# The state-space coefficient moves from B's factors to the powers: one group of transposes, and another order of tables and first products

## The chip, the cores and the metric

The kernel runs on one core of one Trainium2 chip. A core has five engines that run side by side and wait for each other by semaphores: TensorE (PE, matrix products), VectorE (DVE), ScalarE (ACT), GpSimd (POOL) and SyncE (SP, which here only issues DMAs). The metric is the device time of the program in microseconds (us); smaller is better. The three runs of the kernel before took 1129.54, 1130.26 and 1454.06 us; their median is 1130.26 us.

## The reference

A trunk of two layers works on 1024 frames of width 1024. Layer 0 has two branches, a diagonal complex state-space layer (S5) with a GLU, and a retention with eight heads; layer 1 is a convolution module. Each layer is `x = x + mixer(rmsnorm(x))`, and a last RMSNorm follows. The change lies in the S5 part, which for 64 groups of 16 channels and 64 states computes

```
dt = exp(log_dt);  lb = exp((a_re + i a_im) * dt)          # one step of the state
coef = (lb - 1) / (a_re + i a_im)
bb = coef[..., None] * (b_re + i b_im)                     # (64 groups, 64 states, 16 channels)
s_t = lb * s_(t-1) + bb @ u_t                              # over all frames
y_t = Re(c @ s_t) + d * u_t
```

## The kernel before

**Layer 0's front.** `layer0_front` first brings in x, makes its scaled high and low parts (each product of layer 0 is three TensorE products of high and low parts, `mm3`), and computes blocks u0 to u7 of the input projection (`u_block`, 128 columns each, in two halves `mm_u<nb>_0` and `mm_u<nb>_1` of 24 products). Every block is scaled by DVE into a tile `ut` and written to memory as `u_d`. Then come the gate blocks g8 to g23 (`gate_block`, halves `mm_g<nb>_0` and `_1`), and between them the eight blocks B = 0 to 7 of the state-space layer, one for every two gate blocks.

**The state-space layer.** It works in groups of eight frames. `s5_params` makes, on DVE, the powers 0 to 8 of lb (`pr`, `pi`), the rotation factors for longer distances (`e1`, `e2`) and the coefficient (`cfr`, `cfi`); on POOL it makes bb (`s5_bbr`, `s5_bbi`) in six operations named s5bb and s_bb in the profile. `s5_turned` brings the powers and bb into another layout: ACT reorders bb into `hq`, PE transposes three groups of four 128x128 tiles (`turn0` for the powers, `turn1` and `turn2` for bb), ACT copies each group out of PSUM into a tile `turned`, and SP writes it to memory (`pt_d` for the powers, `bt_d` for bb). ACT also copies bb into `bd`, which the products kp read. For each block B, `s5_w2` loads four tiles from there, with rows repeated (PTr and PTi, BTr and BTi, 256 KB each), copies the powers to PSUM (`pw0`, `pw1`) and multiplies them complexly by bb with six DVE operations; the result W2 is what the products `v0`, `v1` of `s5_states` apply to the block's input U (loaded back from `u_d` by `s5_load`). `s5_tables` lets POOL make, in six operations each, W3 (powers times C, read by the products kp and y) and the rotation tables Tc and Ts (read by DVE behind v). `s5_states` issues v and kp and lets DVE add kp and d into Kg; `s5_scan` rotates v on DVE, scans it and rotates it back into S; `s5_out` issues the products y.

**What sets the order.** A scheduler places the instructions of each engine; where the order matters it is written out by hand, as pairs (late, early) of the n-th instruction that writes a named tile: the list `ORDER`, and the pairs that `s5_order` makes for DVE: in each block Kg, then the rotation of v (m0, m1) and the first six operations on v, then the gates and the next block's W2. On PE, `turn1` begins behind the last product of `mm_u6_0`, and v and kp of block 0 stand ahead of the seventh product of `mm_g8_0`. On an engine, and in SP's queue of DMAs, instructions run in order: one that waits holds up all behind it.

**Buffers.** Tiles live in pools that open and close. The pool `ev` (the early pool) holds x, temporaries, bb and the tiles `hq` and `turned`; it is closed after `s5_turned`, and the pool `s5w` of the state-space blocks (U, PT, BT, W2, W3, Tc, Ts and others) takes its place: a tile there waits for the last user of the tile that it lies over. `s5c` lives through the whole front, `mid` through front and retention.

Of the kernel before, what the change touches and what calls it, by code (L numbers as in the profile page):

```python
# [11 lines left out]
F32 = mybir.dt.float32  # L12
# [3 lines left out]
ALU = mybir.AluOpType  # L16
# [3 lines left out]
P = 128  # L20
# [20 lines left out]
ORDER = (  # L41
    ('PE', ('turn1', 0), ('mm_u6_0', 23)),
    ('DVE', ('W2r_0', 0), ('ut_7', 0)),
    ('DVE', ('kraw_3', 0), ('yn_2', 0)),
# [24 lines left out]
    ('PE', ('mm_g9_0', 0), ('kp_0', 7)),  # L69
    ('PE', ('mm_g8_0', 6), ('kp_0', 7)),  # L70
    ('Activation', ('wh_glu2', 0), ('rs_6_0', 0)),
# [13 lines left out]
def s5_order():  # L85

    seq = []
    for b in range(8):
        g, h = 8 + 2 * b, 9 + 2 * b
        turns = [(f"m0_{b}", 0), (f"m1_{b}", 0)]  # L90
        kern = [(f"Kg_{b}", 0), (f"Kg_{b}", 1)]
        z = [(f"v{c}_{b}", n) for n in range(4) for c in range(2)]
        back = [(f"d0_{b}", 0), (f"d1_{b}", 0), *z[6:], (f"S_{b}", 0), (f"S_{b}", 1)]
        w = [(f"{t}_{b + 1}", n) for t, n in (("W2r", 0), ("W2i", 0), ("pw0", 0), ("pw1", 0), ("W2r", 1), ("W2i", 1))]
        w = w if b < 7 else []
        seq += [*kern, *turns, *z[:6]]
        if b:
            seq += [*back, (f"gt_{g}", 0), (f"wl_g{h}", 0), *w[:3], (f"gt_{g}", 1), *w[3:]]
        else:
            seq += [(f"gt_{g}", 0), *w, *back, (f"gt_{g}", 1)]  # L100
        seq += [(f"gt_{h}", 0), *([(f"wl_g{g + 2}", 0)] if b < 7 else []), (f"gt_{h}", 1)]
    return [("PE", ("mm_g8_0", 6), ("v1_0", 7)),
            *(("Activation", (f"pw0_{b + 1}", 0), (f"gt_{8 + 2 * b}", 0)) for b in range(1, 7)),
            *(("DVE", late, early) for early, late in zip(seq, seq[1:]))]
# [33 lines left out]
class Trunk:  # L138
# [208 lines left out]
    def layer0_front(self, st):  # L347
# [144 lines left out]
        self.s5_tab, self.s5_back, self.s5_open, self.s5_last = {}, {}, {}, None  # L492
        for nb in range(3, 6):
            u_block(nb)
        self.s5_turned(ev)
        early.close()
        self.s5 = self.pool("s5w", 1, stack=st)
        self.s5_first = self.s5_load(0)
        for nb in range(6, 8):
            u_block(nb)  # L500
# [153 lines left out]
    def s5_params(self, sp, tp):  # L654
# [162 lines left out]
        with self.tc.issue_after(self.last_phase.ins):  # L817
# [20 lines left out]
            tt(cfi[:], a1[:], rden[:], ALU.mult)  # L838
        self.bb = [tp.tile([P, NP, 16], F32, name=f"s5_bb{c}") for c in "ri"]
        bc = lambda q: q[:].unsqueeze(2).broadcast_to([P, NP, 16])  # L840
# [26 lines left out]
    def s5_turned(self, pool):  # L867


        nc = self.nc  # L870
        self.pt_d = self.dram.tile([2, 2, P, P], F32, name="pt_d")
        self.bt_d = self.dram.tile([2, 4, P, P], F32, name="bt_d")
        fl = lambda t, a, n: t[:, a * n:(a + 1) * n, :].rearrange("p a b -> p (a b)")
        order = [pool.tile([P, 4, P], F32, name=f"hq{c}", tag="sq", bufs=2) for c in range(2)]
        for o, t in zip(order, self.bb):
            nc.scalar.copy(o[:].rearrange("p a (h q) -> p (a h) q", h=4), t[:].rearrange("p q h -> p h q"))
        for i, (dst, parts) in enumerate((
                (self.pt_d[:].rearrange("c a r n -> r (c a) n"), [fl(t, a, 4) for t in (self.pr, self.pi) for a in range(2)]),
                (self.bt_d[0].rearrange("a r n -> r a n"), [order[0][:, a, :] for a in range(4)]),
                (self.bt_d[1].rearrange("a r n -> r a n"), [order[1][:, a, :] for a in range(4)]))):  # L880
            ps = self.bank(f"turn{i}")
            for a, src in enumerate(parts):
                nc.tensor.transpose(ps[:, a * P:(a + 1) * P], src, self.ident[:])
            t = pool.tile([P, 4, P], F32, name=f"turned{i}", tag="xin", bufs=8)
            nc.scalar.copy(t[:].rearrange("p q n -> p (q n)"), ps[:])
            nc.sync.dma_start(dst, t[:])
        for q, t in zip(self.bd, self.bb):
            for g in range(2):
                r = slice(64 * g, 64 * g + 64)
                nc.scalar.copy(q[r, :, 16 * g:16 * g + 16], t[r])  # L890

    def s5_w2(self, B):

        nc, v = self.nc, self.nc.vector
        (ptr, pti), (btr, bti) = ([self.big(f"{n}{c}_{B}", f"{n}{c}", 1) for c in "ri"] for n in ("PT", "BT"))
        dp, db = self.pt_d, self.bt_d

# [22 lines left out]
    def s5_tables(self, B):  # L920
# [8 lines left out]
        pj = lambda t: t[:, :, qs].rearrange("p j q -> p q j").unsqueeze(3).broadcast_to([P, 4, 9, 16])  # L929
        W3 = w.tile([P, 2, 4, 9 * 16], F32, name=f"W3_{B}", tag="W3", bufs=2)  # L930
        made = [self.outer(B, W3[:, 0], W3[:, 1], pj(self.pr), pj(self.pi), bj(self.cr), bj(self.nci), vm,
                           ALU.add, ALU.subtract)]

        Tc, Ts = self.big(f"Tc_{B}", "Tc", 2), self.big(f"Ts_{B}", "Ts", 2)
        vt = lambda ap: ap.rearrange("p q (a b) -> p q a b", b=16)
        ea = lambda t: t[:, 0:8, qs].rearrange("p a q -> p q a").unsqueeze(3).broadcast_to([P, 4, 8, 16])
        eb = lambda t: t[:, 0:16, qs].rearrange("p b q -> p q b").unsqueeze(2).broadcast_to([P, 4, 8, 16])
        made.append(self.outer(B, Tc[:], Ts[:], ea(self.e2[0]), ea(self.e2[1]), eb(self.e1[0]), eb(self.e1[1]), vt))

        self.s5_last = self.chained(chain(*made), self.s5_last)  # L940
        R8 = self.big(f"R8_{B}", "R8", 1)
# [1049 lines left out]
def layout(inp):  # L1991
# [28 lines left out]
    A["s5_prm"] = np.stack([gn(inp["s5_a_re"][0]), gn(inp["s5_a_im"][0]), gn(ldt)], axis=1)  # L2020
    b = lambda a: a.reshape(32, 2, 64, 16).transpose(1, 2, 0, 3).reshape(P, 32, 16)
    c = lambda a: b(a.transpose(0, 2, 1))
    A["s5_br"], A["s5_bi"] = b(inp["s5_b_re"][0]), b(inp["s5_b_im"][0])
# [27 lines left out]
```

## Time and profile before

The profiled execution took 1130.23 us; its profile spans 1128.4 us of that.

| what | value |
|---|---|
| profiled execution, us | 1130.23 |
| its span, us | 1128.4 |
| median of the runs, us | 1130.26 |
| PE busy | 1113.1 us (99%) |
| PE weight load busy | 978.2 us (87%) |
| DVE busy | 816.0 us (72%) |
| ACT busy | 500.2 us (44%) |
| POOL busy | 593.1 us (53%) |
| mean rate of all DMAs | 233 GB/s |

Times in the profile are microseconds from the start of the span; "mean ns" is the duration of one instruction. Matmuls are pipelined, so the distance between two starts, not the duration shown, is what one costs. A row names the line of the kernel, the operation, the tile written and, behind the arrow, the tiles read; buffer and block numbers are left out, so `mm_u` stands for all u blocks. "idle before, releaser" is the time that the engine stood still just before the instruction, and the one that ended it. A DMA's row is its issue; when it has landed is seen from the instructions that waited for it.

### The profile page before, as it was taken

Reading aid. Unit: us, or ns where it says so; the run is one execution under the profiler, and the core shown is the slowest. Engines: PE = TensorE matmul, PEld = TensorE weight load, DVE = VectorE, ACT = ScalarE, POOL = GpSimd, SP = SyncE. Lnnn points to the kernel's source line nnn. Section 1 sums busy time; section 2 is a strip of 40 time slices with the busy share of each in tenths; the row PEclk is TensorE's granted clock in tenths of the full one; section 3 lists DMA queues with packets and bytes.
Section 4 is the critical chain, followed back from the end, with each engine's and each line's share of the span. In section 5 each row is a group of like instructions: output and inputs, shape, how many; then the busy total and the mean of one; then the engine's idle time right before and its main releaser. Section 6 shows DMA issues by size and latency. Waiting matters only on the chain.

```text
span 1128.4 us, 17194 instructions
## 1 busy us (share of the span) xinstructions
PE 1113.1 (99%) x6262; PEld 978.2 (87%) x6262; DVE 816.0 (72%) x1475; ACT 500.2 (44%) x733; POOL 593.1 (53%) x410
## 2 busy tenths in 40 slices
PE   9989999999999999999999999999999999999997
PEld 8877888888888888989888888888888888888886
DVE  6875777776516468586669632599999899999744
ACT  7322433333223232324446523546545677446773
POOL 3058666666137345232574110589544568779863
PEclk9999999999999999999999999999999999999999
DMA  8346555554478766968998998666778655357965
GB/s 314 120 122 206 163 173 183 179 183 163 138 254 272 287 197 193 313 204 301 388 386 300 340 328 288 189 227 206 245 254 288 243 191 177 123 177 243 326 230 188
DMA packets 126501, 262.51 MB, mean 233 GB/s; under 512 B 19792, under 2 KB 50384, under 8 KB 125776
## 3 DMA queue, kind: packets, MB, share of 16 engines
q1 hardware_dynamic: 122960, 248.83, 65.2%
q10 hardware_dynamic: 3456, 12.58, 2.8%
q8 instruction: 49, 0.80, 0.3%
q14 instruction: 36, 0.29, 0.1%
HBM read 182.53 MB, written 74.65 MB: 228 GB/s over the span
## 4 chain that ended last, share of the span: by engine, by line
PE 84%; DVE 6%; DMA 4%; ACT 2%; POOL 2%; issue 2%; SPq 0%; POOLq 0%; DVEq 0%; ACTq 0%
PE mm_g L267 7%; PE mm_g L269 7%; PE mm_g L268 7%; PE mm_wo L269 5%; PE mm_wo L267 5%; PE mm_wo L268 5%; PE mm_b L268 2%; PE mm_a L267 2%; PE mm_a L268 2%; PE mm_b L267 2%; PE mm_b L269 2%; PE mm_a L269 2%; PE mm_oc L268 2%; PE mm_oc L269 2%; PE mm_oc L267 2%
## 5 line engine op out<-in xcount | busy, mean ns | idle before, releaser
L1664 DVE SCALAR_TENSOR_TENSOR cv<-u,convw,cv 128x512 f32<-128x512 f32 x390 | 268.0, 752 | 6.0 <-ACT cv L1631 3.9
L1625 POOL TENSOR_TENSOR tp<-tp,tp 128x512 f32<-128x512 f32 x64 | 82.3, 1287 | 32.8 <-ACT tp L1624 31.9
L267 PE MATMUL mm_g<-xh,wh_g 128*128 128x512 f32 x256 | 97.8, 382 | 0.0
L268 PE MATMUL mm_g<-xl,wh_g 128*128 128x512 f32 x256 | 97.0, 379 | 0.0
L269 PE MATMUL mm_g<-xh,wl_g 128*128 128x512 f32 x256 | 95.9, 379 | 0.0
L529 POOL TENSOR_TENSOR s1q<-s1q,s1q 128x512 f32<-128x512 f32 x12 | 17.2, 1436 | 82.1 <-ACT s1q L524 73.4
L1624 ACT ACTIVATE tp<-u,convw 128x512 f32<-128x512 f32 x64 | 45.3, 718 | 32.4 <-POOL tp L1625 31.6
L478 DVE TENSOR_TENSOR gt<-mm_g,R 128x512 f32<-128x512 f32 x32 | 22.0, 688 | 51.2 <-PE mm_g L269 51.2
L267 PEld LDWEIGHTS mm_g<-xh,wh_g 128*128 128x128 f32 x256 | 48.4, 189 | 7.0 <-issue 0.4
L269 PEld LDWEIGHTS mm_g<-xh,wl_g 128*128 128x128 f32 x256 | 48.4, 189 | 6.8
L268 PEld LDWEIGHTS mm_g<-xl,wh_g 128*128 128x128 f32 x256 | 48.4, 189 | 6.6
L268 PE MATMUL mm_oc<-zl,wh_woc 128*128 128x512 f32 (+1 forms) x144 | 51.4, 357 | 0.2 <-DVE zl L1379 0.2
L267 PE MATMUL mm_oc<-zh,wh_woc 128*128 128x512 f32 (+1 forms) x144 | 51.0, 363 | 0.0
L269 PE MATMUL mm_oc<-zh,wl_woc 128*128 128x512 f32 (+1 forms) x144 | 50.8, 356 | 0.0
L267 PE MATMUL mm_g<-h1h,wh_cg 128*128 128x512 f32 x128 | 48.9, 382 | 0.0
L267 PE MATMUL mm_wo<-ysh,wh_wos 128*128 128x512 f32 x128 | 48.9, 382 | 0.0
L269 PE MATMUL mm_wo<-ysh,wl_wos 128*128 128x512 f32 x128 | 48.6, 380 | 0.3 <-DVE wl_wos L257 0.3
L269 PE MATMUL mm_g<-h1h,wl_cg 128*128 128x512 f32 x128 | 48.5, 379 | 0.0
L268 PE MATMUL mm_wo<-ysl,wh_wos 128*128 128x512 f32 x128 | 48.5, 379 | 0.0
L269 PE MATMUL mm_b<-h1h,wl_cb 128*128 128x512 f32 x128 | 48.5, 379 | 0.0
L267 PE MATMUL mm_a<-h1h,wh_ca 128*128 128x512 f32 x128 | 48.5, 379 | 0.0
L268 PE MATMUL mm_g<-h1l,wh_cg 128*128 128x512 f32 x128 | 48.5, 379 | 0.0
(522 smaller groups left out, 3519.9 us busy)
## 6 DMA issues: line engine op xcount, KB each, us to landing
wf_g<-w_ab SPq DMA_DIRECT2D x16, 512.0 KB
wf_wos<-w_out SPq DMA_DIRECT2D x16, 512.0 KB
wf_wor<-w_out SPq DMA_DIRECT2D x16, 512.0 KB
wf_cb<-w_c SPq DMA_DIRECT2D x16, 512.0 KB
wf_ca<-w_c SPq DMA_DIRECT2D x16, 512.0 KB
wf_woc<-w_out_c SPq DMA_DIRECT2D x16, 512.0 KB
wf_v<-w_v SPq DMA_DIRECT2D x12, 512.0 KB
wf_cg<-w_c SPq DMA_DIRECT2D x11, 512.0 KB
```

Of the source, the lines that this page charges most:

```text
L267: nc.tensor.matmul(ps, wh[:, kb, :], xh, start=start, stop=False, **more)
L268: nc.tensor.matmul(ps, wh[:, kb, :], xl, start=False, stop=False, **more)
L269: self.last_mm = nc.tensor.matmul(ps, wl[:, kb, :], xh, start=False, stop=stop, **more)
L478: nc.vector.tensor_tensor(nat(gt[:, c]), un(ps[:]), nat(self.R[:, c]), op=ALU.mult)
L529: nc.gpsimd.tensor_tensor(a, a, sq[:], op=ALU.add)
L1624: nc.scalar.mul(sk[:], u[:, k:k + HALF], cw[:, nb, k:k + 1])
L1625: gp.tensor_tensor(s0[:], s0[:], sk[:], op=ALU.add)
L1664: v.scalar_tensor_tensor(dst[:], *tap, accs_[i][:], op0=ALU.mult, op1=ALU.add)
```

## The change

The coefficient is multiplied into powers 0 to 7 (`pc`, six DVE operations of 128 x 256 elements) instead of being needed in the turned form of bb. W2 is then (coefficient times power) times b, and b in the turned layout is an input of the program, `s5_bt`, made by the host's layout step from `b_re` and `b_im`; `bt_d`, `hq` and the transposes of bb are gone. bb is still made by POOL, since kp needs it, and moves from `ev` to `s5c`; `turned` moves to `mid`. `s5_turned` and the opening of `s5w` come after block u4 instead of u5 in the program. On PE the four transposes are placed between the halves of u6; v of block 0 comes ahead of the whole of `mm_g8_0`, and kp of block 0 between `mm_g8_0` and `mm_g8_1`. On DVE, W2 of block 0 is no longer tied behind the first half of u7's `ut`, and in block 0 Kg comes behind the first six operations on v. `s5_tables` makes Tc and Ts ahead of W3.

```diff
 ORDER = (
-    ('PE', ('turn1', 0), ('mm_u6_0', 23)),
-    ('DVE', ('W2r_0', 0), ('ut_7', 0)),
+    ('PE', ('turn', 0), ('mm_u6_0', 23)),
+    ('PE', ('mm_u6_1', 0), ('turn', 3)),
+    ('PE', ('mm_g8_0', 0), ('v1_0', 7)),
+    ('PE', ('kp_0', 0), ('mm_g8_0', 23)),
+    ('PE', ('mm_g8_1', 0), ('kp_0', 7)),
...
-    ('PE', ('mm_g8_0', 6), ('kp_0', 7)),
...
-        seq += [*kern, *turns, *z[:6]]
+        seq += [*kern, *turns, *z[:6]] if b else [*turns, *z[:6], *kern]
...
-    return [("PE", ("mm_g8_0", 6), ("v1_0", 7)),
-            *(("Activation", (f"pw0_{b + 1}", 0), (f"gt_{8 + 2 * b}", 0)) for b in range(1, 7)),
+    return [*(("Activation", (f"pw0_{b + 1}", 0), (f"gt_{8 + 2 * b}", 0)) for b in range(1, 7)),
...
-        for nb in range(3, 6):
-            u_block(nb)
+        u_block(3)
+        u_block(4)
         self.s5_turned(ev)
         early.close()
         self.s5 = self.pool("s5w", 1, stack=st)
         self.s5_first = self.s5_load(0)
-        for nb in range(6, 8):
+        for nb in range(5, 8):
             u_block(nb)
...
-        self.bb = [tp.tile([P, NP, 16], F32, name=f"s5_bb{c}") for c in "ri"]
+        self.pc = [tp.tile([P, 8, NP], F32, name=f"s5_pc{c}") for c in "ri"]
+        bc = lambda q: q[:].unsqueeze(1).broadcast_to([P, 8, NP])
+        cmul(self.pc[0][:], self.pc[1][:], pr_[:, :8], pi_[:, :8], bc(cfr), bc(cfi), (8, NP))
+        self.bb = [sp.tile([P, NP, 16], F32, name=f"s5_bb{c}") for c in "ri"]
...
-        self.bt_d = self.dram.tile([2, 4, P, P], F32, name="bt_d")
-        fl = lambda t, a, n: t[:, a * n:(a + 1) * n, :].rearrange("p a b -> p (a b)")
-        order = [pool.tile([P, 4, P], F32, name=f"hq{c}", tag="sq", bufs=2) for c in range(2)]
-        for o, t in zip(order, self.bb):
-            nc.scalar.copy(o[:].rearrange("p a (h q) -> p (a h) q", h=4), t[:].rearrange("p q h -> p h q"))
-        for i, (dst, parts) in enumerate((
-                (self.pt_d[:].rearrange("c a r n -> r (c a) n"), [fl(t, a, 4) for t in (self.pr, self.pi) for a in range(2)]),
-                (self.bt_d[0].rearrange("a r n -> r a n"), [order[0][:, a, :] for a in range(4)]),
-                (self.bt_d[1].rearrange("a r n -> r a n"), [order[1][:, a, :] for a in range(4)]))):
-            ps = self.bank(f"turn{i}")
-            for a, src in enumerate(parts):
-                nc.tensor.transpose(ps[:, a * P:(a + 1) * P], src, self.ident[:])
-            t = pool.tile([P, 4, P], F32, name=f"turned{i}", tag="xin", bufs=8)
-            nc.scalar.copy(t[:].rearrange("p q n -> p (q n)"), ps[:])
-            nc.sync.dma_start(dst, t[:])
+        ps = self.bank("turn")
+        for c in range(2):
+            for a in range(2):
+                nc.tensor.transpose(ps[:, (2 * c + a) * P:(2 * c + a + 1) * P],
+                                    self.pc[c][:, 4 * a:4 * a + 4, :].rearrange("p a b -> p (a b)"), self.ident[:])
+        t = self.mid.tile([P, 4, P], F32, name="turned")
+        nc.scalar.copy(t[:].rearrange("p q n -> p (q n)"), ps[:])
+        nc.sync.dma_start(self.pt_d[:].rearrange("c a r n -> r (c a) n"), t[:])
...
-        dp, db = self.pt_d, self.bt_d
+        dp, db = self.pt_d, self.A["s5_bt"]
...
-        W3 = w.tile([P, 2, 4, 9 * 16], F32, name=f"W3_{B}", tag="W3", bufs=2)
-        made = [self.outer(B, W3[:, 0], W3[:, 1], pj(self.pr), pj(self.pi), bj(self.cr), bj(self.nci), vm,
-                           ALU.add, ALU.subtract)]
...
-        made.append(self.outer(B, Tc[:], Ts[:], ea(self.e2[0]), ea(self.e2[1]), eb(self.e1[0]), eb(self.e1[1]), vt))
-
+        made = [self.outer(B, Tc[:], Ts[:], ea(self.e2[0]), ea(self.e2[1]), eb(self.e1[0]), eb(self.e1[1]), vt)]
+
+        W3 = w.tile([P, 2, 4, 9 * 16], F32, name=f"W3_{B}", tag="W3", bufs=2)
+        made.append(self.outer(B, W3[:, 0], W3[:, 1], pj(self.pr), pj(self.pi), bj(self.cr), bj(self.nci), vm,
+                           ALU.add, ALU.subtract))
...
+    A["s5_bt"] = np.stack([b(inp[f"s5_b_{k}"][0]).transpose(2, 1, 0) for k in ("re", "im")])
```

## The prediction

> **What bounds the kernel now.** I began with the page: the span is 1128.4 us and TensorE (PE) is busy for almost all of it, so only two things can shorten the run: less PE work, or fewer holes on PE. The view of the waits of PE lists the holes, longest total first (us in total, times, longest).
>
> ```profile
> PE turn L883 <- ACT hq L876: 3.1, 2, 2.2
> PE v L966 <- issue: 2.5, 1, 2.5
> ...
> PE rf_ps L558 <- ACT s2q L1829: 0.6, 1, 0.6
> ```
>
> The two largest are in code that this change edits: the transposes of the state-space factors, and the first products with W2. Between the v row and the rf_ps row stand only holes at the very start of the run; behind it nothing reaches 0.6 us. So about 5.7 us of holes are within reach, and past them PE carries the time: whatever PE gains here should arrive at the end. Next the timeline of PE around both holes (start, duration; the brackets give the idle time before it and what ended it).
>
> ```profile
> 79.42 0.38 PE L268 MATMUL mm_u<-xl,wh_u 128*128 128x512 f32 x1
> 82.01 0.66 PE L883 MATMUL turn<-ident,hq 128*128 128x128 f32 x4 [2.22 <-ACT hq L876]
> 82.43 0.46 PE L269 MATMUL mm_u<-xh,wl_u 128*128 128x512 f32 x1
> ...
> 82.94 0.38 PE L268 MATMUL mm_u<-xl,wh_u 128*128 128x512 f32 x1
> 84.24 0.66 PE L883 MATMUL turn<-ident,hq 128*128 128x128 f32 x4 [0.92 <-ACT hq L876]
> 84.65 0.46 PE L269 MATMUL mm_u<-xh,wl_u 128*128 128x512 f32 x1
> ...
> 98.98 0.38 PE L269 MATMUL mm_u<-xh,wl_u 128*128 128x512 f32 x1
> 99.29 0.43 PE L975 MATMUL kp<-W,s_bdr 128*32 128x128 f32 x8
> ...
> 103.31 1.09 PE L966 MATMUL v<-U,W2r 128*64 128x128 f32 x16 [2.53 <-issue]
> 104.20 1.07 PE L966 MATMUL v<-U,W2i 128*64 128x128 f32 x16
> 105.20 0.48 PE L267 MATMUL mm_g<-xh,wh_g 128*128 128x512 f32 x1
> ```
>
> The reader is to see that PE sits still until ScalarE (ACT) has reordered B's factors (hq), once for the real and once for the imaginary part, and later stands for 2.53 us in front of v. What v waited for is in the lists of who reads PT, BT and pw, and in SyncE's (SP's) DMA issues.
>
> ```profile
> L910 ACT COPY pw<-PTr x2: 590/590/590, 92.6 to 103.3; 128x512 f32<-128x512 f32 x2
> L910 ACT COPY pw<-PTi x1: 592/592/592, 94.8 to 94.8; 128x512 f32<-128x512 f32 x1
> L912 DVE TENSOR_TENSOR W2r<-pw,BTr x1: 691/691/691, 97.7 to 97.7; 128x512 f32<-128x512 f32 x1
> L913 DVE TENSOR_TENSOR W2i<-pw,BTi x1: 693/693/693, 100.5 to 100.5; 128x512 f32<-128x512 f32 x1
> ```
>
> ```profile
> 85.97 0.91 SPq L886 DMA_DIRECT2D bt_d<-turned  x2
> 86.97 0.53 SPq L948 DMA_DIRECT2D U<-u_d  x1
> 88.22 0.76 SPq L900 DMA_DIRECT2D PTr<-pt_d  x1
> 89.03 0.60 SPq L900 DMA_DIRECT2D PTi<-pt_d  x1
> 89.74 0.58 SPq L904 DMA_DIRECT2D BTr<-bt_d  x1
> 90.36 0.72 SPq L471 DMA_DIRECT2D u_d<-ut  x1
> 91.18 0.83 SPq L904 DMA_DIRECT2D BTi<-bt_d  x1
> ```
>
> B's turned factors leave at 86, come back behind U, PT and a u_d write, and BTi is there at 100.5 (9.3 us after its issue; PTr took 4.3, PTi 5.8, BTr 8.0). Four more VectorE (DVE) operations of 0.7 us end at 103.3, when v starts. That is the hole of 2.53 us.
>
> **The change, part by part.**
>
> *Eight transposes and four DMA steps less on the chain.* The two groups of four hq transposes, their two hq copies, their two evacuations and the two bt_d writes go. Without them the matmuls from 79.42 to 99.29 would follow each other at their own pace: from 84.65 to 98.98 there are 66 steps in 14.33 us, and without the first, longer one 65 in 14.03, 0.216 us each. From 79.42 to 82.43 stand 3.01 us, from 82.94 to 84.65 1.71 us. Taking one matmul pace of 0.216 from each leaves 2.79 + 1.49 = 4.28 us, and the longer first matmul after each group (0.30 to the next start, against 0.216) adds 0.09 twice: **4.46 us**. Of this 3.14 us are the two holes and 1.3 us the eight transposes. The group that stays (four transposes) has moved from before block u6's first half to behind it; it costs the same in either place, so nothing.
>
> *Are the four transposes late?* They now need the powers times the coefficient: six new DVE operations on 128x256. The nearest rows are the six operations of that shape in the same helper:
>
> ```profile
> 64.90 0.43 DVE L675 TENSOR_TENSOR s5t<-s_e1r 128x256 f32<-128x256 f32 x1
> ...
> 66.57 0.43 DVE L675 TENSOR_TENSOR s_e1i<-s5t,s5t 128x256 f32<-128x256 f32 x1
> 66.91 1.10 DVE L463 TENSOR_TENSOR ut<-mm_u,R 128x512 f32<-128x512 f32 x1
> ```
>
> ```profile
> 64.67 4.56 POOL L257 TENSOR_TENSOR wl_u<-wf_u,wh_u 128x1024 fp32r<-128x1024 f32 x1 [35.19 <-ACT wh_u L256]
> 74.51 1.06 POOL L675 TENSOR_TENSOR s5bb<-s_s_br,s_cfr 128x512 f32<-128x512 f32 x1 [5.28 <-DVE s_cfr L675]
> 75.53 2.08 POOL L675 TENSOR_TENSOR s5bb<-s_s_bi,s_cfr 128x512 f32<-128x512 f32 x1
> ```
>
> ```profile
> L257 POOL TENSOR_TENSOR wl_glu<-wf_glu,wh_glu 128x1024 fp32r<-128x1024 f32 x14 | 33.2, 2378 | 18.8 <-ACT wh_glu L256 16.3 <-DMA yn<-yn_d 2.5
> ```
>
> From 64.90 to 66.91 they took 2.0 us. The coefficient is ready at 74.5 (it releases GpSimd, POOL, there), so the product is ready at 76.5, or 77.6 if one evacuation of ut (1.10) goes first. PE has finished u6's first half at 79.2 less the 0.44 us of the group that no longer precedes it, 78.8. Cover: 1.2 to 2.3 us. Price if that cover is gone: what it is late by.
>
> *v's wait.* New chain: transposes 78.8 to 79.3; ACT's evacuation 0.6 (as the 128x512 copies of pw), 80.0; the write to pt_d, issued then. Its nearest row is bt_d's: the second one, issued within 85.97 to 86.88, was waited for by the row at 89.24 below, so about 2.5 us: landed at 82.8. PTr and PTi are issued at 82.8 and 83.5 and, by the rows above, land after 4.3 and 5.8: 87.1 and 89.3. The copy to pw (0.6) gives 89.9, four operations of 0.7 follow: W2 at **92.7**. By the slowest row (BTi's 9.3 us) PTi lands at 92.8 and W2 is ready at 96.2. PE reaches v at 99.29 - 4.46 = **94.8**. Between a wait of 0 and of 1.4 us I take 0: PT is now issued with less in front of it than PTr and PTi had, since BT no longer depends on any of this.
>
> That BT and U can be early rests on buffers:
>
> ```profile
> 82.07 1.22 POOL L860 TENSOR_TENSOR o<-s_pi,s_s_ci 128x576 f32<-128x576 f32 x1
> ...
> 89.24 1.23 POOL L860 TENSOR_TENSOR o<-s_pi,s_s_cr 128x576 f32<-128x576 f32 x1 [3.29 <-DMA bt_d<-turned]
> ```
>
> POOL's second temporary waited 3.29 us for a DMA out of a turned tile: the state-space pool lies over the early pool's tiles, and those were held by the turned factors. In the changed kernel `turned` lies in the middle pool, which is not reused here, so that wait goes as well, and U, BT and the tables can start as soon as their queue is free.
>
> So the hole of 2.53 us goes. In exchange v stands ahead of kp and of the first g8 matmuls, which were in front of it as cover. They run afterwards, the same number with the same four changeovers, so the sum is unmoved; but v's lateness is now paid in full. Queued behind v's wait on PE: all of g8's first half, 24 x 0.216 = 5.2 us of ready work.
>
> *Tables.* Rotation tables come first, six POOL operations, then W3's six. Even at 1.5 us each, from 82.1 plus 2 us for the collision below, the rotation is made by 93.1 (its reader follows v, over at 96.7) and W3 by 102.1. kp comes behind g8's first half, 96.7 + 5.2 = 101.9: hidden, or at worst 0.2 us. If 1.5 is too much by the 0.27 that 1.23 suggests, 3 us are left over.
>
> *Moved issues.* SP loses two writes of 0.4 to 0.5 us of issue and gains none; the four loads of PT and BT per block stay, BT's only with another source. DVE's six operations (2.0 us) push one evacuation of ut; the product after next needs its bank, 5 us later, so nothing. ACT loses two hq copies and two evacuations. Kg's additions now stand behind the first six operations on v on DVE; kp itself is later than those, so nothing.
>
> *Sum.* 4.46 + 2.53 = 6.99 us. The profiled execution took 1130.23 us around its span of 1128.4, and the median of the runs shown is 1130.26, so either base gives **1123.2 us**.
>
> **The rivals.**
>
> *A, v still waits.* SP issues in the old order, U, PTr, PTi, BTr, a u_d write, BTi, now from 82.8. The old train took from 86.97 to 100.5 and then 2.8 us to v: 82.8 + 13.5 + 2.8 = 99.1, a wait of 4.3 us and 1127.5 us. For it: nothing in the diff orders BT ahead of PT. Against it: SP did not keep the old order of the code elsewhere (a u_d write stands between BTr and BTi), and BT is ready long before PT.
>
> *B, the product and POOL get in each other's way.* The six new DVE operations read two SBUF operands while POOL runs its six products of B. If each had to let one POOL operation pass, they would end at 74.5 + 6 x (1.06 + 0.43) = 83.4; the transposes come 4.6 us late and the time is 1127.8 us. The rows say POOL pays: its wl_u took 4.56 us against 2.378 in the group of 14, 2.2 us more, while DVE's six ran through it at full pace; and s5bb took 2.08 against 1.06. The Trainium skill, "SBUF — State Buffer", section "Who interferes with whom", says that a DVE instruction with two SBUF inputs and a GpSimd instruction that reads SBUF contend, and that the second to issue fully blocks until the first is finished. By that rule POOL's wl_u, issued at 64.67, should have held DVE's operation at 64.90; the trace does not show this, so the rule gets this rival and a small chance.
>
> *C, slower.* One mechanism: SP waits in order. If the u_d write of u7 is put ahead of PT's loads, they go out only after u7 ends at 94.8 and its last half is evacuated (1.10): PTi at 96.5 after its neighbour's issue of 0.6, landed at 102.3, W2 at 105.7, a wait of 10.9 us: 1134.1 us. It turns into a loss as soon as PTi is issued after 92.6 (92.6 + 5.8 + 0.6 + 2.8 = 101.8 = 94.8 + 6.99). For it: v has no cover left. Against it: before, u7's u_d write came behind all of block 0's loads.
>
> *D, gained and given back.* PE arrives 7 us early in a later stage and meets a load or a buffer that did not move, since 6 KB a partition more in longer-lived pools shifts what lies over what. PE's holes after 105 are all 0.6 us or less, but slack is not visible in them. Up to the whole gain: 1123.2 to 1130.2 us, middle 1126.7.
>
> **How the numbers follow.** Forecast (both holes gone, within 1.4 us): 0.60. A 0.16, B 0.07, C 0.06, D 0.08; 0.03 for a gain beyond the sum, which no row supports. The predicted time is the forecast's, 1123.2 us; its own range is 1122.0 to 1124.6. The 8 in 10 range takes in A and most of D and B up to 1127.8, leaving out C and the rest, and 1.7 us below for a run that merely falls low: 1121.5 to 1127.8. A measurement of this kernel can tell about 2% from no change, 22.6 us; every case here is within that: faster by over 2% 0.01, within 0.98, slower 0.01.
>
> **What would show it.** Right: no wait of PE in front of turn, one group of four transposes; v starting near 94.8 straight behind u7; everything after 105 earlier by 7 us. Wrong: a wait at v ended by DVE's W2 or by PT's landing (A, C: look at SP's order around 80 to 96); transposes that wait for DVE (B); a new wait of PE after 105 (D). An unbroken PE with the old end would refute the claim that PE carries the time.

## The result and the profile after

The changed kernel takes 1133.64 us (median of 8 runs, 1131.48 to 1135.9) against 1130.42 us of the kernel before on the same chip (median of 8 runs). The run at 1454.06 us is disturbed and left out of the comparison. The ratio is 1.0032, with a 95% interval of 1.002 to 1.0044: a small loss, where the forecast was a gain of 7 us. The profiled execution took 1132.57 us, 1130.8 us of it in the span. Line numbers of the changed kernel are a little off from those of before (v is line 962, W2's last operations 913).

The page of the profile after shows PE as full as before, at 1116.0 us busy against 1113.1, although eight transposes are gone.

```profile
span 1130.8 us, 17173 instructions
PE 1116.0 (99%) x6254; PEld 980.1 (87%) x6254; DVE 824.5 (73%) x1481; ACT 497.1 (44%) x729; POOL 592.8 (52%) x410
```

Fewer products that take longer: that is the first hint of something besides holes. The view of the waits of PE (us in total, times, longest) has the same two places at its head, with other releasers.

```profile
PE v L962 <- DVE W2r L913: 4.2, 1, 4.2
...
PE turn L879 <- DVE s_pci L676: 1.0, 1, 1.0
PE turn L879 <- DVE s_pcr L676: 0.8, 1, 0.8
```

The transposes wait for the new product of powers and coefficient, 0.8 and 1.0 us, and v waits for W2, now 4.2 us where it had been 2.5. The timeline of PE (start, duration, idle time before it in brackets) shows what lies around both.

```profile
78.52 0.44 PE L879 MATMUL turn<-ident,s_pcr 128*128 128x128 f32 x2 [0.81 <-DVE s_pcr L676]
79.92 0.44 PE L879 MATMUL turn<-ident,s_pci 128*128 128x128 f32 x2 [0.96 <-DVE s_pci L676]
80.12 0.63 PE L268 MATMUL mm_u<-xh,wh_u 128*128 128x512 f32 x1
80.54 0.63 PE L269 MATMUL mm_u<-xl,wh_u 128*128 128x512 f32 x1
...
83.83 0.38 PE L268 MATMUL mm_u<-xh,wh_u 128*128 128x512 f32 x1
...
101.83 1.98 PE L962 MATMUL v<-U,W2r 128*64 128x128 f32 x16 [4.24 <-DVE W2r L913]
103.60 1.92 PE L962 MATMUL v<-U,W2i 128*64 128x128 f32 x16
105.45 0.79 PE L268 MATMUL mm_g<-xh,wh_g 128*128 128x512 f32 x1
...
107.67 0.38 PE L270 MATMUL mm_g<-xh,wl_g 128*128 128x512 f32 x1
...
112.44 0.48 PE L268 MATMUL mm_g<-xh,wh_g 128*128 128x512 f32 x1
```

The reader should look at durations. After the holes before the transposes, a product of u6 lasts 0.63 us instead of 0.38, and the next one starts 0.42 us later instead of 0.216. After the hole before v, sixteen products of v take 1.98 and 1.92 us; in the profile of before the same groups took 1.09 and 1.07. Even g8's first products, up to 107.67, are slow. The windows say why. Behind the start and end of each stand its length, then busy time and count of PE, weight load, DVE, ACT and POOL, then the granted clock (the share of PE's full clock that the chip let through), the DMA share and GB/s.

```profile
81.00:82.00 1.00, 1.00 (x4) 0.82 (x3) 1.00 (x1) 0.95 (x2) 1.00 (x2) 0.50 0.16 50
102.00:103.00 1.00, 1.00 (x12) 1.00 (x14) 1.00 (x2) 0.00 (x0) 1.00 (x2) 0.50 0.50 178
105.30:317.00 211.70, 211.70 (x1454) 184.99 (x1452) 144.95 (x222) 66.63 (x110) 112.84 (x82) 0.99 0.51 166
```

PE is granted half of its clock in both places and counts as fully busy there, so a list of waits cannot show this loss. It costs 1.68 us after the transposes (80.12 to 83.83 is 3.71 us for nine products and a change of operands that take 2.03 at the usual pace) and about 2.8 us after v's hole (from v's start to g8's first product, 101.83 to 105.45, are 3.62 us, where before there were 1.89, and the five products up to 107.67 take 2.22 us instead of 1.17).

The Trainium skill, "TensorE: Matmul & The Clock Gate", section "Part 1: The HAM clock gate (the "warmup" mystery)", says that the array's clock falls to half after at least one idle window of about 3.4 us and returns after a busy one. The trace's record of the granted clock agrees with the window: half clock lasts from 80.29 to 83.70, 3.41 us, and from 100.77 to 107.59, 6.83 us, which is two times 3.41. In all twelve profiles of this case the clock changes only at whole multiples of 3.41 us after its first change. With stretches of 3.41 us marked off from there, the one that ends at 100.77 is idle for 93%, and the next, up to 104.18, is still idle for 31%, as v starts at 101.83; the clock stays at half for one stretch more. The first place does not agree with an idle window: the stretch from 76.87 to 80.29 holds both holes and is idle for only 52%.

The balance closes to 0.2 us. PE begins the second half of g8 at 112.44; in the profile of before it did at 109.84. That is 2.6 us later, and the span is 2.4 us longer. Gained were the 6.99 us forecast, and 1.2 us by which this execution was already ahead at u5 (62.01 against 63.22). That lead is there at u2 and belongs to the execution: over the twelve profiles u5 begins between 61.87 and 63.22, last of all in that of before. Lost were 1.77 (holes at the transposes) + 0.15 (their longer first matmuls) + 1.68 (half clock) + 4.24 (hole at v) + 2.8 (half clock) = 10.6 us. The difference is 2.4 us of the 2.6, and nothing after 112 adds to it.

**Why the product was late.** The forecast had the product of powers and coefficient cost DVE 2.0 us. These are the rows of DVE and then of POOL.

```profile
73.24 0.42 DVE L676 TENSOR_TENSOR s5t<-s_pr,s_cfr 128x256 f32<-128x256 f32 x1
73.58 1.28 DVE L676 TENSOR_TENSOR s5t<-s_pi,s_cfi 128x256 f32<-128x256 f32 x1
...
78.39 1.48 DVE L676 TENSOR_TENSOR s_pci<-s5t,s5t 128x256 f32<-128x256 f32 x1
```

```profile
73.28 1.30 POOL L676 TENSOR_TENSOR s5bb<-s_s_br,s_cfr 128x512 f32<-128x512 f32 x1 [5.26 <-DVE s_cfr L676]
74.54 1.24 POOL L676 TENSOR_TENSOR s5bb<-s_s_bi,s_cfr 128x512 f32<-128x512 f32 x1
```

Both engines are released by the coefficient at 73.2, and from then on each starts one operation per 1.2 us. DVE's six take 6.6 us, from 73.24 to 79.8. In the profile of before a DVE product of the same shape, beside a POOL operation, ran at 0.43 us. The Trainium skill, "SBUF — State Buffer", section "Who interferes with whom", says that a DVE operation with two SBUF inputs contends with a GpSimd operation that reads SBUF, and that the second to issue is blocked. These rows agree with a lock that goes to and fro: from the second on, a DVE operation (1.28 us) lasts as long as POOL's (1.24).

**Why W2 was late.** Here is SP's queue, from the write of the turned powers to the loads that need it, and then the copies on ACT that wait for the loads.

```profile
80.91 0.36 SPq L472 DMA_DIRECT2D u_d<-ut  x1
...
83.07 0.80 SPq L901 DMA_DIRECT2D BTr<-s_bt  x1
83.98 0.38 SPq L883 DMA_DIRECT2D pt_d<-turned  x1
...
90.89 0.61 SPq L897 DMA_DIRECT2D PTr<-pt_d  x1
91.55 0.58 SPq L897 DMA_DIRECT2D PTi<-pt_d  x1
```

```profile
82.32 0.59 ACT L882 COPY turned<-turn 128x512 f32<-128x512 f32 x1
...
97.06 0.59 ACT L907 COPY pw<-PTr 128x512 f32<-128x512 f32 x1 [8.96 <-DMA PTr<-pt_d]
99.28 0.59 ACT L907 COPY pw<-PTi 128x512 f32<-128x512 f32 x1 [1.63 <-DMA PTi<-pt_d]
```

The transposes are over at 80.1, but ACT copies them out at 82.32, behind four copies of bd. SP, in order, issues the write at 83.98, behind a `u_d` write, two other issues and the first load of B. The write has landed at 90.89, when PTr may be issued, 6.9 us later; PTr takes 6.2 us to the copy that waits for it and PTi 7.7. Each step of the chain is late, and v with it.

### The profile page after: what moved, and what is told of

Same layout as the page of the kernel before. It is cut to its first block, busy times and chain, and to the rows that moved or that the text cites. A ratio compares the mean times of both kernels' runs of the same rounds, so it can differ in the third digit from the quotient of the medians.

```text
span 1130.8 us, 17173 instructions
## 1 busy us (share of the span) xinstructions
PE 1116.0 (99%) x6254; PEld 980.1 (87%) x6254; DVE 824.5 (73%) x1481; ACT 497.1 (44%) x729; POOL 592.8 (52%) x410
## 4 chain that ended last, share of the span: by engine, by line
PE 88%; DVE 5%; DMA 3%; ACT 1%; issue 1%; POOL 1%; SPq 0%; POOLq 0%; ACTq 0%; DVEq 0%
PE mm_g L268 7%; PE mm_g L269 7%; PE mm_g L270 7%; PE mm_wo L268 5%; PE mm_wo L270 5%; PE mm_wo L269 5%; PE mm_b L269 2%; PE mm_b L270 2%; PE mm_a L269 2%; PE mm_a L268 2%; PE mm_b L268 2%; PE mm_a L270 2%; PE mm_oc L269 2%; PE mm_oc L270 2%; PE mm_oc L268 2%; PE mm_glu L268 2%
## 5 line engine op out<-in xcount | busy, mean ns | idle before, releaser
L1621 POOL TENSOR_TENSOR tp<-tp,tp 128x512 f32<-128x512 f32 x64 | 82.5, 1289 | 33.4 <-ACT tp L1620 32.5
L269 PE MATMUL mm_u<-xl,wh_u 128*128 128x512 f32 x128 | 48.8, 385 | 0.0
```

Source lines behind the costliest of these rows:

```text
L269: nc.tensor.matmul(ps, wh[:, kb, :], xl, start=False, stop=False, **more)
L1621: gp.tensor_tensor(s0[:], s0[:], sk[:], op=ALU.add)
```

## Experiments

**1. v behind the first half of g8.** Only PE's order of block 0 is changed; everything else is the changed kernel.

```diff
-    ('PE', ('mm_g8_0', 0), ('v1_0', 7)),
-    ('PE', ('kp_0', 0), ('mm_g8_0', 23)),
+    ('PE', ('v0_0', 0), ('mm_g8_0', 23)),
+    ('PE', ('v1_0', 0), ('mm_g8_0', 23)),
+    ('PE', ('kp_0', 0), ('v1_0', 7)),
```

> Changed kernel, but on PE v of block 0 and then kp stand between the two halves of g8, instead of v ahead of the first half. Theory (the loss is PE's holes, and each hole is paid a second time by the half clock that follows it): the 5.2 us of the first half cover the hole of 4.2 us in front of v, so that hole and the second stretch of half clock (2.8 us) both go: 1133.6 - 7.0 = 1126.6 us. Rival 1 (the clock is a bystander, only the hole counts): 1129.4 us. Rival 2 (a later stage gives the gain back): 1133.6 us.

Measured: 1125.91 us (5 runs), against 1131.01 of the kernel before; ratio 0.9956 [0.9944, 0.9969]. The timeline of PE has no hole in front of v:

```profile
101.86 1.09 PE L963 MATMUL v<-U,W2r 128*64 128x128 f32 x16
```

W2 is no earlier than in the change; the 5.2 us of g8's first half stand in front of it instead of behind. That is worth 7.7 us beside the change's 1133.64, somewhat more than hole and half clock of its profile together (4.24 + 2.8 = 7.0). (The change itself was not run again beside the experiments. The kernel before, which was, took 0.3 to 0.6 us more there than the 1130.42 us above, so gains "beside the change" are uncertain by about that much.) The two holes at the transposes are there as before, but in this profile no half clock follows them; its window of 81 to 82 has the granted clock at 1.00, in the column behind the busy times:

```profile
81.00:82.00 1.00, 1.00 (x7) 0.89 (x6) 1.00 (x2) 0.82 (x3) 1.00 (x2) 1.00 0.00 0
```

**2 and 3. PE kept busy during the hole.** In front of v, products of a constant tile with itself are written into v's own bank, and v overwrites their result; W2 is as late as in the change. With 36 of them first:

```diff
+    ('PE', ('v0_0', 0), ('mm_u7_1', 23)),
...
+            for _ in range(36 if B == 0 and c == 0 else 0):
+                nc.tensor.matmul(ps[:, :P], self.ones[:], self.ones[:], start=True, stop=True)
```

> Changed kernel, plus 36 idle products of 128x128 on PE between the last product of u7 and v, about 4.0 us of work whose result v overwrites. The wait for W2 stays as it is; only the idleness goes. Theory: the clock stays full behind the wait, so 2.8 us come back: 1130.8 us. Rival 1 (the half clock has another cause, or is a matter of the records): 1133.6 us, or more if the idle products run past W2.

Measured: 1133.21 us (12 runs), ratio 1.0019 [1.001, 1.0028]. The filling was mis-sized: the timeline shows 8.20 us of it, where 4.0 were meant (each of the 36 stands there as two records), so it ended at 106.6, some 3 us after W2 was ready, and the time could not decide. The profile does show v at full clock behind the filling.

```profile
98.48 8.20 PE L961 MATMUL v<-ones 128*128 128x128 f32 x72
106.61 1.09 PE L965 MATMUL v<-U,W2r 128*64 128x128 f32 x16
```

With 18 (the only other edit is `range(18`):

```diff
+            for _ in range(18 if B == 0 and c == 0 else 0):
```

> Changed kernel, plus 18 idle products between u7 and v; the 36 of the run before took 8.2 us, so 18 should take 4.1 us and end just as W2 is ready. The wait stays, PE is only not idle in it. Theory (half clock follows an idle PE): v and the first products of g8 run at full clock, the distance from the first product of v to kp is 7.3 us instead of 10.0, and 2.8 us come back: from 3.2 to 0.4 us above the kernel before. Rival (the clock falls for another reason): still 3.2 us above it, distance 10.0 us.

Measured: 1130.13 us (10 runs) against 1130.72, ratio 0.9991 [0.9981, 1.0001].

```profile
97.51 4.18 PE L961 MATMUL v<-ones 128*128 128x128 f32 x36
101.62 1.09 PE L965 MATMUL v<-U,W2r 128*64 128x128 f32 x16
...
108.89 0.43 PE L974 MATMUL kp<-W,s_bdr 128*32 128x128 f32 x8
```

v starts at 101.62, as in the change (101.83), and from its start to kp are 7.27 us instead of 10.04. Work without any use in the hole saves 2.8 us in the profile and 3.5 us by the medians (1133.64 to 1130.13). The mean granted clock of the runs says the same: 0.994 to 0.996 in the change's eight, 0.999 in seven of these ten. So the slow products follow from PE's idleness before them, and are no property of v or of its operands. (The profiled run, 1132.13 us, is the slowest of the ten. There a later wait of 1.65 us, for the scores of the retention, is followed by 3.41 us of half clock as well, from 487.3.)

**4. The product ahead of POOL.** Four copies of single elements make POOL's products of bb wait until DVE has made the product, and ACT copies the turned powers ahead of the bd copies.

```diff
+        for q in x2:
+            gp.tensor_copy(q[:, 0, 0, 0:1], self.pc[1][:, 0, 0:1])
+            gp.tensor_copy(q[:, 1, 0, 0:1], self.pc[1][:, 0, 0:1])
...
-                nc.scalar.copy(q[r, :, 16 * g:16 * g + 16], t[r])
+                with self.tc.issue_after(turned.ins):
+                    nc.scalar.copy(q[r, :, 16 * g:16 * g + 16], t[r])
```

> Changed kernel, but POOL's products of B wait until DVE has finished the coefficient times the powers (four tiny POOL copies read its last element first), and ACT copies the transposed powers out of PSUM ahead of the four copies into bd. Theory (collision of DVE and POOL): the six DVE operations take 2.0 us instead of 6.6, the transposes no longer wait (1.8 us) and the first stretch of half clock goes (1.7 us); the write to pt_d starts some 4 us earlier and so does W2, so the hole in front of v stays about as long: 1133.6 - 3.5 = 1130.1 us. Rival (the DMA queue sets W2, whatever starts when): W2 stays at 101.8, the hole grows by what PE gained, 1133.6 us.

Measured: 1130.45 us (11 runs), ratio 0.9997 [0.9987, 1.0006]. A row of DVE, one of PE, one of SP's waits and one of SP's issues:

```profile
75.86 0.42 DVE L676 TENSOR_TENSOR s_pci<-s5t,s5t 128x256 f32<-128x256 f32 x1
```

```profile
78.48 0.38 PE L882 MATMUL turn<-ident,s_pcr 128*128 128x128 f32 x2
```

```profile
SPq L905 <- POOL s_bbi L676: 4.5, 1, 4.5
```

```profile
85.32 0.37 SPq L886 DMA_DIRECT2D pt_d<-turned  x1
```

Without POOL beside it, DVE takes 0.42 us again, the product is there at 76.3, the transposes wait for nothing and no half clock follows them. This is the forecast's front part, and it is worth 3.2 us beside the change. But the powers, copied out of PSUM by 79.7, are then written at 85.32: SP stood 4.5 us with BTr at its head, whose buffer lies over a temporary of POOL's products. v still waits 4.9 us; this hole brings one stretch of half clock (99.52 to 102.94) and not two, and from v's start to kp are 8.94 us, 1.7 more than in experiment 3.

**5. The write of the powers ahead of the loads.** SP issues pt_d ahead of U and B of block 0.

```diff
-        self.s5_first = self.s5_load(0)
+        with self.tc.issue_after(self.pt_write.ins):
+            self.s5_first = self.s5_load(0)
...
-        with self.tc.issue_after(self.u_load.ins) if B else nullcontext():
+        with self.tc.issue_after((self.u_load if B else self.pt_write).ins):
```

> Changed kernel, but in SP's queue the write to pt_d goes ahead of the loads of U and BT of block 0, and U of block 1 behind PT of block 0. Theory (the write stood behind 1 MB of loads that nobody needed yet, 83.98 to 90.9): the write lands 2.5 us after its issue, PTi lands near 94 instead of 99.2, W2 is ready near 97.5, the hole in front of v is under 0.5 us and the second half-clock stretch goes: 1133.6 - 7.0 = 1126.6 us. Rival (all these bytes have to pass before W2 anyway): W2 within 1 us of 101.8, 1133.6 us.

Measured: 1128.86 us (11 runs), ratio 0.9979 [0.997, 0.9988]; the gain beside the change is 4.8 us of the 7.0 expected. In the profile v waits 0.29 us and keeps its clock, and the slow stretch after the transposes is still there. PE begins g8's second half 6.0 us earlier than in the change, and the span is 4.0 us shorter: 2.0 are given back, 0.9 of it to a longer wait in the retention (1.1 us where the change has 0.2). From SP's issues and PE's timeline:

```profile
83.65 0.36 SPq L884 DMA_DIRECT2D pt_d<-turned  x1
...
88.14 0.58 SPq L898 DMA_DIRECT2D PTr<-pt_d  x1
```

```profile
98.60 1.09 PE L963 MATMUL v<-U,W2r 128*64 128x128 f32 x16 [0.29 <-DVE W2r L914]
```

The write goes out at about the same time as in the change, but PTr can be issued 4.5 us after it instead of 6.9.

**6. The kernel before, with v between g8's halves.** This asks what the order of experiment 1 is worth without the change.

```diff
-    return [("PE", ("mm_g8_0", 6), ("v1_0", 7)),
+    return [("PE", ("v0_0", 0), ("mm_g8_0", 23)), ("PE", ("v1_0", 0), ("mm_g8_0", 23)), ("PE", ("mm_g8_1", 0), ("v1_0", 7)),
```

> The kernel before, with one thing of its order changed: v of block 0 between the two halves of g8 instead of behind g8's first three products. Theory (PE carries the time): its hole of 2.5 us in front of v is covered and nothing else moves: 2.5 us below the kernel before (ratio 0.998). Rival (a later wait takes it back): no difference.

Measured: 1128.86 us (11 runs), ratio 0.9981 [0.9972, 0.999], close to the expected: 1.9 us of v's 2.53 by the medians. The profile holds a second reading. A hole of 2.21 us at the transposes, as long as that of before (2.22), is followed by half clock here, which the profile of before did not have (a row of PE's timeline and a window, the clock again behind the busy times):

```profile
81.25 0.66 PE L883 MATMUL turn<-ident,hq 128*128 128x128 f32 x4 [2.21 <-ACT hq L876]
```

```profile
82.00:85.00 3.00, 2.56 (x9) 1.75 (x8) 0.00 (x0) 2.94 (x5) 2.92 (x3) 0.50 0.00 0
```

So holes of about 2 us bring it in some executions and not in others. The kernel before pays it in many of its runs too: the profile of before, with full clock from 6.5 us to its last product, has a mean clock of 0.999, and of the 68 runs of that kernel beside the experiments 43 have 0.997 or less, as none of experiments 1, 7 and 10 has. One stretch of 3.41 us takes 0.0015 off the mean.

**7. All three: experiments 1, 4 and 5.**

```diff
+    ('PE', ('v0_0', 0), ('mm_g8_0', 23)),
...
+            gp.tensor_copy(q[:, 0, 0, 0:1], self.pc[1][:, 0, 0:1])
...
+        with self.tc.issue_after(self.pt_write.ins):
```

> Changed kernel with all three edits: POOL's products of B behind the coefficient's product and ACT's copy of the powers first; the write to pt_d first in SP's queue; v and kp between the halves of g8. Theory: no hole of PE is left in this stretch and the clock stays full, so the forecast's sum comes true: 4.46 + 2.53 = 7.0 us below the kernel before (ratio 0.9938, about 1124 us beside 1131). Rival (v's order alone does it, the rest is covered or is given back): the same as with v's order alone, ratio 0.9956, 5 us below.

Measured: 1123.14 us (1121.88 to 1123.72, 5 runs), ratio 0.9933 [0.9921, 0.9946]. It is the fastest version, and within 0.1 us of the time forecast for the change. PE has no hole between 40 and 105. Two waits grew later:

```profile
PE mm_glu L269 <- ACT gu L1483: 1.1, 1, 1.1
...
PE ro L1341 <- DVE sc L1318: 0.8, 1, 0.8
```

The first is in no list of waits of before or after, the second was 0.3 us before. PE began g8's second half at 101.92, 7.9 us earlier than before, and the span is 6.5 us shorter: 1.4 us are given back, and these two waits are longer by 1.6.

**8. Experiments 4 and 5, v first as in the change.** If both repairs of the chain bring W2 in time, the change's own order of PE should do as well as that of experiment 7.

```diff
+            gp.tensor_copy(q[:, 0, 0, 0:1], self.pc[1][:, 0, 0:1])
...
+        with self.tc.issue_after(self.pt_write.ins):
```

> Changed kernel with the product first and the write to pt_d first, but v ahead of g8 as in the change. Theory: the write goes out at 79.8 and lands at 82.5, but BTr stands ahead of PT in SP's queue and waits for POOL until 84.4; PTi goes out at 86.5, lands 5.8 us later, W2 is ready at 95.7, PE arrives at 94.6: a hole of 1.1 us, too short for the half clock, 5.9 us below the kernel before (ratio 0.9948). Rival (PT needs 7.3 us as in the run with the write first): W2 at 97.2, a hole of 2.6 us, 4.4 us below (0.9961).

Measured: 1128.75 us (10 runs), ratio 0.9984 [0.997, 0.9998]. Theory and rival both missed. From the issues of SP and the timeline of PE:

```profile
78.91 0.36 SPq L887 DMA_DIRECT2D pt_d<-turned  x1
...
83.60 0.80 SPq L906 DMA_DIRECT2D BTr<-s_bt  x1
```

```profile
98.13 1.09 PE L967 MATMUL v<-U,W2r 128*64 128x128 f32 x16 [4.33 <-DVE W2r L918]
```

The write leaves 5 us earlier than in the change, and v starts only 3.7 us earlier and waits 4.33 us, with one stretch of half clock behind it (99.13 to 102.54). The loads are what is slow: BTr waited for POOL again until 83.60, and W2 came 14.5 us after it. Setting the profiles side by side gives a regularity. The four loads PTr, PTi, BTr and BTi form a train, and v or W2's end follows the first of them, whichever it is, by 15.0 us in before (88.22 to 103.2), 16.2 in experiment 6, 15.0 in 4, 13.9 in 5, 15.3 in 7 and 14.5 in 8. (In the change it is 18.7, and 17.7 to 18.7 in experiments 1 to 3, as PT's loads wait in the middle of the train for the slow write.) B's factors from an input or from a written tile make little difference to that: the change took two writes away and left the train as long as it was.

**9. B's factors of block 0 out of the train.** They are loaded into tiles of their own before u3, and the loads of block 1 go behind PT of block 0; otherwise as the change.

```diff
+        self.bt0 = [self.mid.tile([P, 4, P], F32, name=f"B0{c}") for c in "ri"]
+        for c, bt in enumerate(self.bt0):
+            nc.sync.dma_start(bt[:].rearrange("p q n -> p (q n)"),
...
-            for c, bt in enumerate((btr, bti)):
+            for c, bt in enumerate((btr, bti) if B else ()):
```

> Changed kernel, but B's factors of block 0 lie in tiles of their own in the middle pool and are loaded before u3, and the loads of block 1 (U, PT, BT) go behind PT of block 0; the product, POOL and PE's order stay as in the change. Theory (the four loads with repeated rows form a train of 14 to 15 us, wherever B's come from, so W2 comes that long after the first of them): with two of the four out of it, the write to pt_d lands 2.5 us after its issue, PTr and PTi take 4.3 and 5.8 us as before, W2 is ready near 96, and there is no hole in front of v: 7.0 us less than the change, 3.5 below the kernel before (ratio 0.997). Rival (it was the place of the write to pt_d alone): PT still lands 9 us after its issue, W2 near 100, a hole of 2 to 3 us: about 1 us below the kernel before.

Measured: 1127.27 us (7 runs) against 1130.76, ratio 0.9967 [0.9956, 0.9979], as the theory gave, but by luck of the parts: W2 was ready at 97.8 instead of the 96 expected, and v waited 2.10 us instead of not at all, while the half clock behind the transposes, which the theory had left in, is missing in that profile. From PE's timeline and SP's waits:

```profile
97.83 1.09 PE L970 MATMUL v<-U,W2r 128*64 128x128 f32 x16 [2.10 <-DVE W2r L920]
```

```profile
SPq L904 <- DMA pt_d<-turned: 5.1, 1, 5.1
```

From PTr's issue at 88.45 to W2's real part it took 9.3 us, where the train of four took 14 to 16. But PTr waited 5.1 us in SP's queue for the write to land.

**10. The same, with experiments 4 and 5.** The change's order of PE is kept.

```diff
+        self.bt0 = [self.mid.tile([P, 4, P], F32, name=f"B0{c}") for c in "ri"]
...
+            gp.tensor_copy(q[:, 0, 0, 0:1], self.pc[1][:, 0, 0:1])
...
+        with self.tc.issue_after((self.pt_write if B == 0 else self.pt_load if B == 1 else self.u_load).ins):
```

> As the run before, and the product first and the write to pt_d first; v still ahead of all of g8, as in the change. Theory: the write goes out at 79 and lands at 81.5, PTi lands at 88, W2 is ready near 91, PE arrives at 94: no hole, no half clock, and the forecast's sum comes true with the change's own order on PE: 7.0 us below the kernel before (ratio 0.9938). Rival (PT is slow by itself, as in the run with the chain only, 9 us): W2 at 94 to 95, a hole of about 0.5 us: 6.5 below; if U's load in front of PT is what takes the time, W2 at 97 and 4 below.

Measured: 1123.99 us (1122.62 to 1124.79, 5 runs), ratio 0.9941 [0.9927, 0.9955], the expected value. From the views of SP, DVE and PE:

```profile
78.80 0.36 SPq L893 DMA_DIRECT2D pt_d<-turned  x1
...
83.23 0.62 SPq L909 DMA_DIRECT2D PTr<-pt_d  x1
```

```profile
92.10 0.68 DVE L926 TENSOR_TENSOR W2i<-W2i,pw 128x512 f32<-128x512 f32 x1
```

```profile
93.62 1.09 PE L975 MATMUL v<-U,W2r 128*64 128x128 f32 x16
```

W2 is there at 92.8, 0.8 us before PE comes to v, and v goes straight on at full clock. So the design of the change works, with v first, when the product, the write and B's loads are all out of each other's way. Here too the end gets less than the stretch gives: g8's second half begins 8.4 us earlier than before, and the span is 5.4 us shorter. Of the 8.4 the lead at u5 is 1.2 (62.01 against 63.22), so the change is worth 7.2 of them. The waits of PE that grew behind are those of the GLU's products (1.2 and 0.8 us, none before) and of the retention (0.8 instead of 0.3).

## Why the prediction was wrong, by its own steps

**Right.** *Eight transposes and four DMA steps less*: the 4.46 us came, and v's 2.53 with them, wherever neither holes nor slow stretches were left. From u5's first product to g8's second half PE needs 46.62 us before, 39.46 in experiment 10 and 39.26 in experiment 7: 7.2 and 7.4 us less, where 6.99 were forecast. That the times of 7 and 10 land on the forecast as well is in part luck. By an estimate from the mean clocks in experiment 6 (43 of 68 runs, 1.7 us each) the kernel before loses about 1 us to half clock, which the forecast did not count, and 1.4 and 3.0 us are given back later. *v's lateness is now paid in full*: experiment 1 gives it cover again and takes 7.7 us off. *Tables*: kp waited for nothing, so making W3 last stayed hidden. *PE carries the time*: the change's 2.6 us at the end of the stretch are 2.4 us at the end of the run. The claim holds less well for gains: what experiments 7 and 10 gave back is rival D in small.

**Wrong, the step "Are the four transposes late?"** It had the product made in 2.0 us, since "the rows say POOL pays". It took 6.6 us and both paid. That is rival B's mechanism, at 1.1 us a DVE operation (6.6 by 6) where B had put 1.49; it began at 73.24 and not at 74.5, and cost 1.77 us of holes and not 4.6. The failure was to argue from two rows of POOL, wl_u and an s5bb, and to leave out what DVE did just behind:

```profile
67.92 1.36 DVE L811 COPY s_e2r<-s_e1r 128x32 f32<-128x32 f32 x1
69.19 0.17 DVE L812 COPY s_e2i<-s_e1i 128x32 f32<-128x32 f32 x1
```

The first of two like copies takes 1.36 us instead of 0.17 and ends with POOL's wl_u at 69.2; all twelve profiles show it. So DVE paid there too. wl_u ends 2.3 us after DVE's products do, at 66.91, about its usual length of 2.38: it may have stood still until then, in which case this trace does follow the rule that rival B rests on, with DVE first. This is argued, not shown. Experiment 4, with the product alone, shows operations of 0.42 us and on-time transposes. What makes one pair run through and the other alternate is not settled.

**Wrong, the step "v's wait".** Four terms were too small (and a slip of 0.3: 80.0 and 2.5 make 82.5, not 82.8). ACT's evacuation was put at the end of the transposes and came 2.2 us later. The write was to be "issued then", and was issued 1.1 us after ACT's copy ended, with BTr's issue in front. It was to land after "about 2.5 us"; PTr could go out 6.9 us later, and in experiments 4, 5, 9 and 10 between 4.3 and 5.6. And PTr and PTi were to take 4.3 and 5.8 us "with less in front of it"; they took 6.2 and 7.7. The sentence that BT "can start as soon as their queue is free" overlooked that its buffers lie over the temporaries of POOL's products: BTr waited for s_bbi in experiments 4, 7 and 8 and held up SP's whole queue. A v that waits 4.3 us was rival A, and the size of the hole agrees (4.24), by luck: PE came to v at 97.6 instead of 94.8 and W2 at 101.8 instead of 99.1, both some 2.7 us late. Its mechanism, the old train of loads again, is right in part: BTr even went ahead of the write of the powers, which no rival had. Rival C's 1134.1 us is near the measured time by luck too: its mechanism did not occur, as PTr and PTi went out at 90.89 and 91.55, ahead of the next write of u_d at 92.23.

**Missing altogether: what a hole costs besides its length.** The sum and all rivals counted a wait by its duration. Each of the two waits was followed by a stretch of half clock, together 4.5 us, which neither the waits nor the busy share show. With the two holes in the sum but without these 4.5 us, the time would have been 1123.2 + 4.24 + 1.77 + 0.15 = 1129.4 us, a small gain; with them it is 1133.9, and 1133.64 was measured. Experiments 1 and 3 bear this out: cover for the hole at v takes back 7.7 us, useless work in it 3.5. The price is not fixed: holes of 4.86 and 4.33 us in experiments 4 and 8 cost 1.7 and 1.6 us more, as one stretch of half clock followed and not two. Besides, A and B were weighed as if only one could come true; both did.

**Open.** Whether a hole of about 2 us is followed by half clock goes with its place among the stretches of 3.41 us, worked out for each profile from the changes of its clock. In the change and in experiments 2, 3 and 5 one stretch holds both holes at the transposes and is idle for 52%, in experiment 6 one holds the hole of 2.21 us (65%), and the clock falls. In experiments 1 and 9 a boundary cuts the second hole, no stretch is idle for more than 42 and 45%, and the clock stays. Idle time is not the whole rule: 53% in the profile of before and 56% ahead of v in experiment 8 brought no fall, and 48% in experiment 3, near 487, did. What counts as work there was not tried. Why each load with repeated rows takes so long was not tried apart; while only such loads move (102 to 103 in the change's profile), the 16 DMA engines are busy for half of the time on average, at 178 GB/s. Experiments 4, 5 and 8 gain 3.2, 4.8 and 4.9 us beside the change; that 8 does not gain the sum fits the train that starts when POOL lets BTr go, but was not tried by itself. What makes the start differ by up to 1.35 us from execution to execution is open too.

## What to carry to other kernels

When ready work is moved from in front of a dependent product to behind it, time the whole chain to that product from its worst rows, queue by queue (who is in front on ACT, who on SP, which buffer a load lies over), because every microsecond of lateness is then paid, and a hole of 4 to 5 us on PE cost between a third and two thirds as much again in slow products after it (1.6 to 2.8 us). Look at the granted clock by windows and at the duration of the products beside the list of waits. And before replacing a written tile by an input, see which part of the loading takes the time: here it was the loading itself, not the wait for the data.

## What the hardware showed that was not expected

- PE at half clock after holes, in stretches of 3.41 us: two behind 4.24 us of idleness (100.77 to 107.59), one behind 0.81 + 0.96 us with a pair of transposes between (80.29 to 83.70). Busy shares count such stretches as full.
- The granted clock changes only at whole multiples of 3.41 us after its first change, in all twelve profiles; whether a hole of about 2 us is paid for depends on how these stretches cut it.
- DVE and POOL in lockstep: six products of 128x256 on DVE, 0.42 us each alone, at one per 1.2 us beside POOL's products of 128x512, which themselves lasted 1.24 us instead of 1.06.
- Four loads of 256 KB with repeated rows take 14 to 16 us from the first issue where nothing holds them up in between, two of them 9.0 to 9.3 us (experiments 10 and 9), up to the end of the DVE operation that completes W2's real part.
- A write of 256 KB, from its issue until a load of the same data could be issued, took 4.3 to 7.3 us (experiments 4 and 1); what makes the difference was not tried apart.
